# A two-layer mLSTM, attention and RWKV-7 trunk on one core: values mixed behind the 16x16 inverse, odd chunks and state products in the other column half

## The chip, the core and the metric

The kernel runs on one core of a Trainium2 chip. Its engines are TensorE (PE, with its weight loads as PEld), VectorE (DVE), ScalarE (ACT), GpSimd (POOL) and SyncE (SP), which here mainly issues DMAs. The metric is the device time of one execution in microseconds, as the median of several runs.

## What is computed

Two layers, each of one input projection, three branches and one output projection, on 512 tokens of 2048 features in float32:

```python
for l in range(2):
    h = rms_norm(x, norm_g[l]);  proj = h @ w_in[l]
    y_ml  = mlstm(4 heads of 128, chunks of 64)      # from columns mq mk mv mo mz
    y_mla = low-rank attention(8 heads of 128 + 64)  # from columns cq ck az
    y_rw  = rwkv7(8 heads of 64)                     # from columns rr rk rv rz and "misc"
    x = x + concat(silu(z) * y for the three) @ w_out[l]
return rms_norm(x, final_norm_g)

# the branch that is changed:
def step(S, inp):                 # per head, S is 64x64
    rt, wt, kt, vt, at, bt = inp
    sa = einsum('bhvk,bhk->bhv', S, at)
    S = S * wt + sa * bt + vt * kt
    return S, einsum('bhvk,bhk->bhv', S, rt)
v = v if l == 0 else v + (v_first - v) * sigmoid(v0 + (v @ v1) @ v2)
y = head_layer_norm(y) + sum(r * k * r_k) * v
```

## The kernel before

Projections and their fill. The input projection of a layer is 26 blocks of 256 columns (`ORDER`, `gemm`, L239; L235 for mv). Each float32 weight tile is split by ACT and DVE into a high and a low part (`wsplit`, L150 and L151), and three passes of 128x128 by 512 columns (256 for mv) are summed. The results go to DRAM (`park`) and are fetched again by their users. `Work.along` calls one step of these projections for every step (`yield`) of a branch, so that the branches' code and the projections' code alternate; the order of each engine's instructions is then made when the program is built, by a scheduler that simulates it. Inside `with in_order()` PE's instructions keep the order of the code. On the chip each engine runs its queue strictly in that order.

Pairs. `rw_pair(p)` handles two of the eight RWKV heads, in eight chunks of 64 tokens, four pairs a layer. It makes decays and keys; a head sum psbo (L714) for the bonus term bv; on POOL the products bk (L785); the values v, in layer 1 mixed with those of layer 0 by a product psv2, a sigmoid and a second fetch; their transposes psTv into UV; the transposes psTa into AR; the 64x64 products psG and transposes psTk into GG. The lower triangular 64x64 matrices of the chunks are then inverted. The 16x16 diagonal blocks are inverted on DVE, reached through two DMA round trips (`inv_d`), which ends with T32 and X32 (L898, L903). Then 32x32 blocks: psQ and psT (L913, in `prod32`), psQ and psX again (L940, L949), each a group of small PE matmuls, an evacuation by ACT or DVE, and the next group. psR (L842) is issued with the first psQ. psW, psM, psN and psY (L842, L851) make the pair's state terms.

Small tiles. A matmul whose operands are 32 or 64 rows and columns uses a tile of PE: rows by where the operands start, columns by where the output starts. `prod32` and `prod` use the tiles on the diagonal. `cross` sends the odd chunks to the other column half and therefore into a second PSUM bank; before, psR, psW and psM are made so.

States and heads. After the pairs, `rw_states` runs the recurrence over chunks (psS, L995), then for each pair the product psYl (L1015), the norm and the transposes psTy. It alternates with `ml_head(0)` and `ml_head(1)` of the mLSTM branch (psSm L1085, psN L1099, psHT L1130). `ml_head(2)` and `ml_head(3)` alternate with the attention's low-rank steps (psrck, psrcq). Then attention (`HEADS`: psqr, psqn, pskn, psv, pssc, pspt, pso) and the output projection (po, L1390).

PSUM has eight banks by tag: two "a" (`bank`), two "b" (`bank2`, of which a head's psN holds both), three "g" (projections), one "h" (`bank3`).

Of the kernel before, what the change touches and what calls it, by code (L numbers as in the profile page):

```python
# [73 lines left out]
def trunk(ctx, tc, a, out):  # L74
    nc = tc.nc
# [441 lines left out]
    for l in range(DEPTH):  # L517
# [176 lines left out]
        def rw_pair(p, l=l):  # L694
# [13 lines left out]
            def head_sum(x, tag, name):  # L708
# [3 lines left out]
                ps = bank(f"{name}{nm}")  # L712
# [47 lines left out]
            ps = head_sum(bo, "AR", "psbo")  # L760
# [3 lines left out]
            v = fetch("rv")  # L764
            if l > 0:
                bg.ensure("rv1")
                ps = bank(f"psv2_{nm}")
                mm(ps, lhsT=v2[:, p * 128:(p + 1) * 128], rhs=kept["vv"], start=True, stop=True)
                yield
                s = tmp("vs")  # L770
                sigm(s, ps, pch(R_V0 + p))
                vf = tmp("vf")
                dma(vf, vf_d[p])
                tt(vf, vf, v, ALU.subtract)
                tt(vf, vf, s, ALU.mult)
                tt(v, v, vf, ALU.add)
            tt(bv, bv, v, ALU.mult)
            dma(tail_d[p, 0], bv)
# [11 lines left out]
            def token_major(blocks, dst, nn, bank_=bank):  # L790
# [5 lines left out]
                for par in range(2):  # L796
                    for h in range(2):
# [5 lines left out]

            UV = rp.tile([128, 2, 8, 64], F32, tag="UV", name=f"UV{nm}")
            token_major(lambda tb: v[:, tb * 128:(tb + 1) * 128], lambda h: UV[hs[1 - h], h], "v")
            AR = rp.tile([128, 8, 128], F32, tag="AR", name=f"AR{nm}")
            token_major(lambda tb: ar[:, 0, 2 * tb:2 * tb + 2, :].rearrange("p c n -> p (c n)"),
                        lambda h: AR[hs[h], :, 0:64], "a", bank2)
# [17 lines left out]
            for half in range(2):  # L826
                ps = bank(f"psTk{half}{nm}")
                for c in range(4):
# [3 lines left out]
                    GG[:, :, half * 4:half * 4 + 4, 128:192], ps.rearrange("p (c h n) -> p h c n", h=2, n=64))  # L832
            yield
            def cross(n, lhs, rhs, name, banks_):
# [4 lines left out]
                for c in range(0, 8, 2):  # L839
                    for odd in (1, 0):  # L840
# [64 lines left out]
            for _ in range(3):  # L905
                yield

            def prod32(lhs, rhs, name):
                ps = bank(f"{name}{nm}")
                pv = ps[:, 0:256].rearrange("p (c n) -> p c n", n=32)  # L910
                for c in range(8):
                    for n, q in enumerate(q4):
                        mm(pv[q, c, :], lhsT=lhs(q, c, n), rhs=rhs(q, c), start=True, stop=True)  # L913
                return pv

            def blk(m):
                return lambda q, c, e=0: m[q, c, :]
            Q = small([128, 8, 32], "Q", "Qa")
            with in_order():
                psQ = prod32(lambda q, c, n: GG[q, n // 2, c, n % 2 * 32:n % 2 * 32 + 32], blk(T32), "psQ")  # L920
# [620 lines left out]
```

## Time and profile before

| | us |
|---|---|
| median of 3 runs | 1999.47 (1997.14 to 2000.08) |
| the profiled execution | 2003.1 |
| its span, first to last instruction | 2001.4 |
| PE busy | 1953.5 (98%) |
| DVE busy | 1234.5 (62%) |
| ACT busy | 861.5 (43%) |
| POOL busy | 136.2 (7%) |

Busy is the share of the span in which an engine had an instruction in work. Matmuls overlap with their successors, so what a matmul costs is the distance from its start to the next one's. The granted clock of PE stands in the slices of the page and in each window. A wait is the idle time of an engine ahead of an instruction, with the instruction that ended it.

### The profile page before, as it was taken

What the parts mean: (1) busy time and instruction counts of PE and PEld (TensorE: products, weight loads), DVE (VectorE), ACT (ScalarE), POOL (GpSimd) and SP (SyncE); (2) the same over time, 40 slices, a digit from 0 to 9 for tenths busy, and PEclk for the clock granted to TensorE, in tenths of its full rate; (3) what the DMA queues carried; (4) which work ended last, traced back from release to release, by engine and by line L of the source; (5) the groups of instructions that cost most, each with busy time, mean ns of one, the idle gap of its engine ahead of it and who ended that gap; (6) DMA issues with size and microseconds to landing.
All of it is one profiled execution on the core that took longest, in us unless ns stands there. A gap on an engine that the chain in (4) does not pass through costs nothing.

```text
span 2001.4 us, 31675 instructions
## 1 busy us (share of the span) xinstructions
PE 1953.5 (98%) x12544; PEld 1622.1 (81%) x12544; DVE 1234.5 (62%) x2115; ACT 861.5 (43%) x1483; POOL 136.2 (7%) x168
## 2 busy tenths in 40 slices
PE   8999999999999999999999999999999998799998
PEld 6888888888888878888887788888888877687886
DVE  6864867575666499533365458567664768785343
ACT  6534343434546355323353234242423566554233
POOL 4010101100000021000001001010100001110000
PEclk9999999999999999999999999999999999899999
DMA  5443434335555443344444443434345555233334
GB/s 175 136 132 115 121 117 127 111 106 169 162 177 173 124 118 122 101 137 135 144 116 135 127 111 117 127 117 132 109 121 163 169 172 168 76 121 122 116 116 158
DMA packets 246393, 264.86 MB, mean 132 GB/s; under 512 B 49972, under 2 KB 178174, under 8 KB 246246
## 3 DMA queue, kind: packets, MB, share of 16 engines
q1 hardware_dynamic: 245398, 261.88, 42.9%
q8 instruction: 98, 1.61, 0.3%
q0 software_dynamic: 848, 0.97, 0.2%
q14 instruction: 49, 0.40, 0.1%
HBM read 212.45 MB, written 50.35 MB: 131 GB/s over the span
## 4 chain that ended last, share of the span: by engine, by line
PE 87%; DVE 6%; DMA 2%; issue 2%; ACT 2%; SPq 0%; ACTq 0%; DVEq 0%
PE po L1390 17%; PE pg_az L239 7%; PE pg_rr L239 4%; PE pg_mo L239 4%; PE pg_rz L239 4%; PE pg_rk L239 4%; PE pg_rv L239 4%; PE pg_mz L239 4%; PE pg_cq L239 4%; PE pg_mv L235 4%; PE pg_mq L239 3%; PE pg_mk L239 3%; PE pssc L1311 2%; PE pg_ck L239 2%; PE pg_misc L239 2%
## 5 line engine op out<-in xcount | busy, mean ns | idle before, releaser
L1390 PE MATMUL po<-whi_o,mh 128*128 128x512 f32 x512 | 200.3, 391 | 0.1
L1390 PE MATMUL po<-whi_o,ml 128*128 128x512 f32 x512 | 199.4, 389 | 0.0
L151 DVE TENSOR_TENSOR wlo_o<-raw_o,whi_o 128x1024 fp32r<-128x1024 f32 x64 | 78.3, 1224 | 188.4 <-ACT whi_o L150 187.3
L1390 PE MATMUL po<-wlo_o,mh 128*128 128x512 f32 x512 | 187.8, 390 | 0.0
L150 ACT ACTIVATE whi_o<-raw_o 128x1024 fp32r<-128x1024 f32 x64 | 67.7, 1059 | 204.6 <-PE po L1390 166.3
L1390 PEld LDWEIGHTS po<-whi_o,mh 128*128 128x128 f32 x512 | 96.1, 188 | 20.5 <-DVE Vl L254 0.6
L1390 PEld LDWEIGHTS po<-wlo_o,mh 128*128 128x128 f32 x512 | 96.1, 188 | 19.9
L1390 PEld LDWEIGHTS po<-whi_o,ml 128*128 128x128 f32 x512 | 96.1, 188 | 19.6
L239 PE MATMUL pg_az<-xh,whi_az 128*128 128x512 f32 x256 | 101.5, 397 | 0.0
L239 PE MATMUL pg_az<-xl,whi_az 128*128 128x512 f32 x256 | 100.9, 394 | 0.0
L239 PE MATMUL pg_az<-xh,wlo_az 128*128 128x512 f32 x256 | 100.0, 396 | 0.0
L235 PE MATMUL pg_mv<-wlo_mv,xh 128*128 128x256 f32 x256 | 73.2, 286 | 1.4 <-DVE wlo_mv L151 1.4
L235 PE MATMUL pg_mv<-whi_mv,xl 128*128 128x256 f32 x256 | 72.9, 285 | 0.0
L235 PE MATMUL pg_mv<-whi_mv,xh 128*128 128x256 f32 x256 | 72.6, 284 | 0.0
L785 POOL TENSOR_TENSOR bk<-kk,Ei 64x512 f32<-64x512 f32 x16 | 27.5, 1717 | 443.3 <-DVE E L730 230.6
L239 PEld LDWEIGHTS pg_az<-xh,wlo_az 128*128 128x128 f32 x256 | 48.5, 190 | 9.7
L239 PEld LDWEIGHTS pg_az<-xh,whi_az 128*128 128x128 f32 x256 | 48.6, 190 | 9.6
L239 PEld LDWEIGHTS pg_az<-xl,whi_az 128*128 128x128 f32 x256 | 48.6, 190 | 9.5
L151 DVE TENSOR_TENSOR wlo_az<-raw_az,whi_az 128x1024 fp32r<-128x1024 f32 x32 | 39.1, 1222 | 20.6 <-ACT whi_az L150 20.3
L239 PE MATMUL pg_rk<-xl,whi_rk 128*128 128x512 f32 x128 | 51.6, 404 | 0.0
L239 PE MATMUL pg_rk<-xh,whi_rk 128*128 128x512 f32 x128 | 51.0, 402 | 0.5 <-ACT xh L252 0.5
L239 PE MATMUL pg_cq<-xh,whi_cq 128*128 128x512 f32 x128 | 51.2, 400 | 0.0
(572 smaller groups left out, 5548.9 us busy)
## 6 DMA issues: line engine op xcount, KB each, us to landing
raw_o<-in_w_out_dram SPq DMA_DIRECT2D x64, 512.0 KB
raw_az<-in_w_in_dram SPq DMA_DIRECT2D x32, 512.0 KB
raw_rk<-in_w_in_dram SPq DMA_DIRECT2D x16, 512.0 KB
raw_rr<-in_w_in_dram SPq DMA_DIRECT2D x16, 512.0 KB
raw_rv<-in_w_in_dram SPq DMA_DIRECT2D x16, 512.0 KB
raw_rz<-in_w_in_dram SPq DMA_DIRECT2D x16, 512.0 KB
raw_mq<-in_w_in_dram SPq DMA_DIRECT2D x16, 512.0 KB
raw_mk<-in_w_in_dram SPq DMA_DIRECT2D x16, 512.0 KB
```

The lines of the kernel that those rows point to most:

```text
L150: act(hi, raw, AF.Copy)
L151: (nc.gpsimd if name[0] == "u" or name in ("misc0_0", "misc0_1") else nc.vector).tensor_tensor(lo, raw, hi.bitcast(F32), ALU.subtract)
L235: mm(ps[u][:, (tb % 2) * 256:(tb % 2) * 256 + 256], lhsT=xx[:, sl], rhs=w[:, i, :], start=(k == 0 and n == 0 and tb % 2 == 0), stop=(k == ...
L239: mm(ps[u], lhsT=w[:, i, u * 128:(u + 1) * 128], rhs=xx, start=(k == 0 and n == 0), stop=(k == 15 and n == 2))
L785: nc.gpsimd.tensor_tensor(bk[q, :, slot, :], x[q].rearrange(c64, t=64), Ei[q].rearrange(c64, t=64), ALU.mult)
L1311: mm(ps[:, 0:n], lhsT=x1[:, ts_], rhs=x2[:, 0:n], start=(j == 0), stop=(j == 5))
L1390: mm(pss[tb], lhsT=xx[:, sl], rhs=w, start=(k == korder[0] and j == 0), stop=(k == korder[15] and j == 2))
```

## The change

- The value fetch, the layer 1 value mix, bv times v, and the transposes psTv move from ahead of bk to behind the 16x16 inverse (behind the first `flip()`). psTa moves behind psTk.
- psbo is put into the bank of tag "h" instead of "a".
- `prod32` becomes `cross32`: the odd chunks go to the column half that their row half doesn't use, in a second bank. The evacuations are split into even and odd chunks; the odd ones move between partition halves, for psT through a tile "back".
- psQ and psX of the second 32x32 step likewise, their evacuation now half on ACT and half on DVE.
- psYl, before on the diagonal, likewise, with a "b" bank for the odd chunks, in the order of chunks 2, 1, 4, 3, 6, 5, 7, inside `in_order()`.
- psW issues even chunks before odd ones.

```diff
-            ps = head_sum(bo, "AR", "psbo")
+            ps = head_sum(bo, "AR", "psbo", bank3)
             yield
             bv = tmp("bv")
             nc.scalar.copy(bv, ps)
-            v = fetch("rv")
-            if l > 0:
...
-            tt(bv, bv, v, ALU.mult)
-            dma(tail_d[p, 0], bv)
...
-            UV = rp.tile([128, 2, 8, 64], F32, tag="UV", name=f"UV{nm}")
-            token_major(lambda tb: v[:, tb * 128:(tb + 1) * 128], lambda h: UV[hs[1 - h], h], "v")
...
             flip()
-            for _ in range(3):
+            yield
+            v = fetch("rv")
+            if l > 0:
+                bg.ensure("rv1")
+                ps = bank(f"psv2_{nm}")
+                mm(ps, lhsT=v2[:, p * 128:(p + 1) * 128], rhs=kept["vv"], start=True, stop=True)
                 yield
...
+            UV = rp.tile([128, 2, 8, 64], F32, tag="UV", name=f"UV{nm}")
+            token_major(lambda tb: v[:, tb * 128:(tb + 1) * 128], lambda h: UV[hs[1 - h], h], "v")
+            for _ in range(2):
+                yield
...
+            def cross32(rows, lhs, rhs, name, banks_, order=(1, 0)):
+                pv = [b_(f"{name}{o}{nm}")[:, 0:128].rearrange("p (c n) -> p c n", n=32) for o, b_ in enumerate(banks_)]
+                for c in range(0, 8, 2):
+                    for o in order:
+                        for i, j in rows:
+                            mm(pv[o][q4[j ^ 2 * o], c // 2, :], lhsT=lhs(i, c + o), rhs=rhs(i, c + o),
+                               start=True, stop=True)
                 return pv
...
-            tt(Q, psQ, mq.rearrange("p a b -> p (a b)")[:, None, :].broadcast_to([128, 8, 32]), ALU.mult)
+            for j in range(2):
+                tt(Q[hs[j], odd, :], psQ[1][hs[1 - j]], mqb[hs[1 - j]], ALU.mult)
+            tt(Q[:, even, :], psQ[0], mqb, ALU.mult)
...
-            psT_ = prod32(blk(X32), blk(Q), "psT32")
-            tt(T32, psT_, T32, ALU.add)
+            with in_order():
+                psT_ = cross32(four, lambda i, c: X32[q4[i], c, :], lambda i, c: Q[q4[i], c, :], "psT32", (bank, bank))
+            back = small([128, 4, 32], "back")
+            for j in range(2):
+                nc.scalar.copy(back[hs[j]], psT_[1][hs[1 - j]])
+            tt(T32[:, even, :], psT_[0], T32[:, even, :], ALU.add)
+            tt(T32[:, odd, :], back, T32[:, odd, :], ALU.add)
...
-            for h in range(2):
-                nc.scalar.copy(Q[q4[2 * h + 1]], pv[q4[2 * h + 1]])
+            for j in (1, 3):
+                nc.scalar.copy(Q[q4[j], odd, :], psQ[1][q4[j ^ 2]])
+                nc.vector.tensor_copy(Q[q4[j], even, :], psQ[0][q4[j]])
...
-                psY = bank(f"psYl{nm}").rearrange("p (c n) -> p c n", n=64)
-                for c in range(1, 8):
-                    for q in hs:
-                        mm(psY[q, c, :], lhsT=Yl[q, c, :], rhs=DNa[q, c - 1, p, :], start=True, stop=True)
+                psY = [b_(f"psYl{o}{nm}").rearrange("p (c n) -> p c n", n=64) for o, b_ in enumerate((bank, bank2))]
+                with in_order():
+                    for c in (2, 1, 4, 3, 6, 5, 7):
+                        for h, q in enumerate(hs):
+                            mm(psY[c % 2][hs[h ^ c % 2], c, :], lhsT=Yl[q, c, :], rhs=DNa[q, c - 1, p, :],
+                               start=True, stop=True)
```

How this moves instructions, at four places. The names are tile, pair or head, and a buffer number.

PE at layer 1's entry into attention, before: pg_az is the layer's last projection, psHT_2 belongs to mLSTM head 2, psrcq to the low-rank queries.

```order
L239 MATMUL pg_az_15726<-xh_15_8291,wlo_az_3_15791 128x512
L1248 MATMUL psqr_0_15868<-cqh_0_14934,whi_uqr_0_15821 128x512
...
L1248 MATMUL psqr_0_15868<-cqh_3_14937,wlo_uqr_0_15822 128x512
L1130 MATMUL psHT_2_15162<-idf,hn_2_15157 128x128
L1203 MATMUL psrcq_15055<-ones,cqr_1_15049 128x1 x4
L1130 MATMUL psHT_2_15162<-idf,hn_2_15157 128x128 x3
L1248 MATMUL psqn_0_15902<-cqh_0_14934,whi_uqk_0_15864 128x512
```

The same place after the change, here with head 3's transposes (psHT_3).

```order
L239 MATMUL pg_az_15974<-xl_13_8429,whi_az_3_16038 128x512
L1145 MATMUL psHT_3_15555<-idf,hn_3_15550 128x128
L239 MATMUL pg_az_15974<-xh_13_8413,wlo_az_3_16039 128x512
L1145 MATMUL psHT_3_15555<-idf,hn_3_15550 128x128 x3
L239 MATMUL pg_az_15974<-xh_14_8414,whi_az_3_16038 128x512
...
L239 MATMUL pg_az_15974<-xh_15_8415,wlo_az_3_16039 128x512
L1263 MATMUL psqr_0_16116<-cqh_0_15182,whi_uqr_0_16069 128x512
```

Head 2's end and all of head 3 stood behind the last projection; now both heads end ahead of it, with six projections between head 3 and psqr.

PE between the head sum psbo and psG in pair 1 of layer 0, before.

```order
L714 MATMUL psbo_1_1807<-psbox_1_1804,bones 128x512
L794 MATMUL psTv_1_1842<-idf,xrv_1_1830 128x128 x4
L714 MATMUL psbo_1_1807<-psbox_1_1804,bones 128x512
L239 MATMUL pg_mq_2523<-xh_0_132,whi_mq_0_2426 128x512
L239 MATMUL pg_mq_2523<-xl_0_148,whi_mq_0_2426 128x512
```

And after.

```order
L714 MATMUL psbo_1_1746<-psbox_1_1743,bones 128x512
L239 MATMUL pg_rv_2355<-xh_8_140,whi_rv_2_2435 128x512
L797 MATMUL psG_1_1807<-ar_1_1732,bk_1_1769 128x128
L797 MATMUL psG_1_1806<-ar_1_1732,bk_1_1769 128x128
L797 MATMUL psG_1_1807<-ar_1_1732,bk_1_1769 128x128
```

psTv has left the place between psbo and psG, and psG, which stood 22 projections later, follows psbo directly.

PE at the second 32x32 step (psQ) of pair 0 in layer 0, before: one bank, one row of 16.

```order
L239 MATMUL pg_rr_1861<-xl_2_150,whi_rr_0_1765 128x512
L239 MATMUL pg_rr_1861<-xh_2_134,wlo_rr_0_1766 128x512
L239 MATMUL pg_rr_1861<-xh_3_135,whi_rr_0_1765 128x512
L940 MATMUL psQ_0_1524<-T_0_1332,GG_0_1178 32x32 x16
L239 MATMUL pg_rr_1861<-xl_3_151,whi_rr_0_1765 128x512
```

And after, with one buffer number for the odd and one for the even chunks.

```order
L239 MATMUL pg_rk_1671<-xl_5_153,whi_rk_1_1675 128x512
L919 MATMUL psQ_0_1447<-T_0_1202,GG_0_1060 32x32 x2
L919 MATMUL psQ_0_1446<-T_0_1202,GG_0_1060 32x32 x2
L919 MATMUL psQ_0_1447<-T_0_1202,GG_0_1060 32x32 x2
L919 MATMUL psQ_0_1446<-T_0_1202,GG_0_1060 32x32 x2
```

The 16 matmuls stand in one uninterrupted group as before, odd and even chunks by turns.

DVE at the first psQ of pair 3 in layer 1, before: wlo is the low part of a projection's weights.

```order
L151 TENSOR_TENSOR wlo_cq_0_14645<-raw_cq_0_14612,whi_cq_0_14644 128x1024
L923 TENSOR_TENSOR Qa_3_12751<-psQ_3_12754,mq 128x256
L926 COPY AR_3_12547<-psR_3_12788 64x4x64
L542 TENSOR_TENSOR sg_cq_0_14660<-pg_cq_14550,rb_9554 128x512
L929 TENSOR_TENSOR T_3_12697<-psT_3_12822,T_3_12697 128x256
L903 STREAM_TRANSPOSE X_3_12698<-T_3_12697 128x256
```

And after.

```order
L151 TENSOR_TENSOR wlo_mo_3_14597<-raw_mo_3_14564,whi_mo_3_14596 128x1024
L931 TENSOR_TENSOR Qa_3_12854<-psQ_3_12858,mq 64x4x32 x2
L932 TENSOR_TENSOR Qa_3_12854<-psQ_3_12857,mq 128x4x32
L935 COPY AR_3_12713<-psR_3_12892 64x4x64
L942 TENSOR_TENSOR T_3_12766<-psT_3_12941,T_3_12766 128x4x32
L943 TENSOR_TENSOR T_3_12766<-back_3_12976,T_3_12766 128x4x32
L886 STREAM_TRANSPOSE X_3_12767<-T_3_12766 128x256
```

One operation on psQ became three, one on psT two, behind the same kind of wlo operation.

## Rows read from the trace of the kernel before

**Rows 1.** The page: busy us (share of the span) by engine; granted clock in slices.

```profile
PE 1953.5 (98%) x12544; PEld 1622.1 (81%) x12544; DVE 1234.5 (62%) x2115; ACT 861.5 (43%) x1483; POOL 136.2 (7%) x168
PEclk9999999999999999999999999999999999899999
```

**Rows 2.** The page: the chain that ended last, shares by engine.

```profile
PE 87%; DVE 6%; DMA 2%; issue 2%; ACT 2%; SPq 0%; ACTq 0%; DVEq 0%
```

**Rows 3.** Windows: start:end, length, busy (instructions) PE PEld DVE ACT POOL, clock, DMA.

```profile
698.00:747.00 49.00, 45.79 (x253) 38.65 (x252) 45.03 (x90) 28.37 (x62) 15.04 (x9) 0.97 0.43 122
1673.00:1749.00 76.00, 59.03 (x310) 47.68 (x309) 60.29 (x131) 44.99 (x99) 15.48 (x9) 0.89 0.38 116
...
1640.00:1652.00 12.00, 9.04 (x41) 7.39 (x40) 8.55 (x14) 7.12 (x11) 0.00 (x0) 0.72 0.48 155
```

**Rows 4.** Timeline of PE at both layers' entry into attention: start us, length.

```profile
698.18 0.39 PE L239 MATMUL pg_az<-xl,whi_az 128*128 128x512 f32 x1
698.41 0.39 PE L239 MATMUL pg_az<-xh,wlo_az 128*128 128x512 f32 x1
698.63 0.39 PE L1248 MATMUL psqr<-cqh,whi_uqr 128*128 128x512 f32 x1
...
746.92 0.39 PE L1248 MATMUL psqn<-cqh,whi_uqk 128*128 128x512 f32 x1
...
1673.21 0.39 PE L239 MATMUL pg_az<-xh,wlo_az 128*128 128x512 f32 x1
...
1748.98 0.39 PE L1248 MATMUL psqn<-cqh,whi_uqk 128*128 128x512 f32 x1
```

**Rows 5.** Waits of PE: us in total, times, longest.

```profile
PE psv L1276 <- DVE qrf L1221: 5.0, 2, 2.6
PE pskn L1248 <- DVE Vl L254: 4.4, 1, 4.4
PE psHT L1130 <- DVE hn L1126: 3.6, 1, 3.6
...
PE psT L913 <- DVE Qa L923: 2.7, 3, 1.1
PE psN L1099 <- DVE mel L254: 2.2, 1, 2.2
...
PE psrck L1175 <- ACT cksq L1170: 0.7, 1, 0.7
```

**Rows 6.** Timeline of PE in layer 0, head 3; 12 psN stand from 641.67.

```profile
640.86 0.95 PE L1203 MATMUL psrcq<-ones,cqr 128*128 128x1 f32 x8
641.67 0.31 PE L1099 MATMUL psN<-mvh,meh 128*128 128x130 f32 x1
...
643.04 0.39 PE L1085 MATMUL psSm<-mqh,mkh 128*128 128x384 f32 x1
```

**Rows 7.** Timeline of weight loads, four groups of small tiles: start, length, passes.

```profile
156.38 0.64 PEld L913 LDWEIGHTS psQ<-T,GG 32*32 32x32 f32 x64 [0.35 <-issue]
...
157.06 0.56 PEld L842 LDWEIGHTS psR<-UV,GG 64*64 64x64 f32 x32
...
165.09 0.58 PEld L940 LDWEIGHTS psQ<-T,GG 32*32 32x32 f32 x32 [0.35 <-DVE wlo_rr L151]
...
527.35 0.90 PEld L1015 LDWEIGHTS psYl<-DN,Yl 64*64 64x64 f32 x28 [0.17 <-issue]
```

**Rows 8.** Groups by line: busy us, mean ns of one, idle ahead.

```profile
L923 DVE TENSOR_TENSOR Qa<-psQ,mq 128x256 f32<-128x256 f32 x8 | 3.4, 421 | 2.0 <-PE psQ L913 2.0
...
L961 DVE COPY UV<-psW 64x256 f32<-64x256 f32 x8 | 3.3, 418 | 5.8 <-ACT UV L960 5.8
...
L151 DVE TENSOR_TENSOR wlo_o<-raw_o,whi_o 128x1024 fp32r<-128x1024 f32 x64 | 78.3, 1224 | 188.4 <-ACT whi_o L150 187.3
```

**Rows 9.** Timeline of POOL and PE in pair 2 of layer 0: start, length.

```profile
304.78 3.85 POOL L785 TENSOR_TENSOR bk<-kh,Ei 64x512 f32<-64x512 f32 x2
...
309.13 0.39 PE L714 MATMUL psbo<-psbox,bones 128*128 128x512 f32 x1
```

More of the change, by code (lines that the diff above doesn't have):

```diff
@@ L706, in rw_pair, with head_sum @@
             inv_d = inv_ds[p]
-            def head_sum(x, tag, name):
+            def head_sum(x, tag, name, bank_=bank):
                 hl = rp.tile([128, 2, T], F32R, tag=tag, name=f"{name}x{nm}")
                 split2(hl[:, 0], hl[:, 1], x)
-                ps = bank(f"{name}{nm}")
+                ps = bank_(f"{name}{nm}")
                 for u in range(2):
@@ L839, in cross @@
                 for c in range(0, 8, 2):
-                    for odd in (1, 0):
+                    for odd in order:
                         for h in (1, 0):
@@ new lines, in rw_pair @@
+            v = fetch("rv")
[3 more added lines that the diff above has]
+                mm(ps, lhsT=v2[:, p * 128:(p + 1) * 128], rhs=kept["vv"], start=True, stop=True)
+                yield
+                s = tmp("vs")
+                sigm(s, ps, pch(R_V0 + p))
+                vf = tmp("vf")
+                dma(vf, vf_d[p])
+                tt(vf, vf, v, ALU.subtract)
+                tt(vf, vf, s, ALU.mult)
+                tt(v, v, vf, ALU.add)
@@ L918, in rw_pair @@
+            four = [(i, i) for i in range(4)]
             Q = small([128, 8, 32], "Q", "Qa")
+            mqb = mq.rearrange("p a b -> p (a b)")[:, None, :].broadcast_to([128, 4, 32])
             with in_order():
-                psQ = prod32(lambda q, c, n: GG[q, n // 2, c, n % 2 * 32:n % 2 * 32 + 32], blk(T32), "psQ")
+                psQ = cross32(four, lambda i, c: GG[q4[i], i // 2, c, i % 2 * 32:i % 2 * 32 + 32],
+                              lambda i, c: T32[q4[i], c, :], "psQ", (bank, bank))
@@ L929, in rw_pair @@
-            tt(T32, psT_, T32, ALU.add)
+            for j in range(2):
+                tt(Q[hs[j], odd, :], psQ[1][hs[1 - j]], mqb[hs[1 - j]], ALU.mult)
+            tt(Q[:, even, :], psQ[0], mqb, ALU.mult)
+            nc.scalar.copy(AR[:, even, 64:128], psR[0])
+            nc.scalar.copy(AR[hs[0], odd, 64:128], psR[1][hs[1]])
+            nc.vector.tensor_copy(AR[hs[1], odd, 64:128], psR[1][hs[0]])
+            yield
+            with in_order():
+                psT_ = cross32(four, lambda i, c: X32[q4[i], c, :], lambda i, c: Q[q4[i], c, :], "psT32", (bank, bank))
@@ L957, in rw_pair @@
             with in_order():
-                W = cross(128, lambda h, c: X[hs[h], c, :], lambda h, c: AR[hs[h], c, :], "psW", (bank, bank2))
-            even, odd = slice(0, 8, 2), slice(1, 8, 2)
+                W = cross(128, lambda h, c: X[hs[h], c, :], lambda h, c: AR[hs[h], c, :], "psW", (bank, bank2), (0, 1))
             nc.scalar.copy(UV[hs[0], 0, odd, :], W[1][hs[1], :, 64:128])
```

62 lines of the change are left out of this document (21 added, 41 removed).

## The prediction

> **What bounds the kernel now.** I read the page's first lines, then the chain that ended last, then TensorE (PE) by stretch and the waits of PE. PE is busy 98% of the span and holds 87% of the chain [rows 1, 2]: a projection matmul of 512 columns follows the one before it every 0.227 us (698.18, 698.41, 698.63 in [rows 4]), and the work of a head pair stands between such matmuls, so that its latency costs nothing while projections are left to issue. Two things can therefore shorten the time: fewer PE nanoseconds in the pair work itself, and PE waits where the projections have run out. The reader should look for the second first. Both layers enter attention with the same work: from the last projection matmul (az) to the fourth group psqn. In layer 0 that is 698.41 to 746.92, 48.51 us; in layer 1 it is 1673.21 to 1748.98, 75.77 us [rows 4]. The stretch of layer 1 has PE idle for 17.0 of 76 us against 3.2 of 49 us in layer 0, and a mean granted clock of 0.89 against 0.97 [rows 3]: between its two levels, 2.4 and 1.2 GHz, 0.89 means about 17 of 76 us at the lower one. The long waits are named: 4.4 us for Vl, 3.6 us for hn, once each, and for qrf 5.0 us in two places, one in each layer [rows 5]. The first two are there because heads 2 and 3 of the mLSTM branch still run when layer 1 has no projection left; the 57 more matmuls of that stretch [rows 3] are theirs.
>
> **The change, part by part. 1: the order at the end of layer 1.** The counts in this part are matmuls in the order in which the program stands, which the ordered rows ahead of this text show in pieces. Before, 494 projection matmuls of layer 1 stand behind the last state product (psY) of its last pair; none is left at head 2's psHT, so head 2's end and all of head 3 stand among the attention's first products. After, 709 are left at that psY, 154 at head 2's psHT and 7 at head 3's. So 215 matmuls, 215 x 0.227 = 49 us of cover, move from the pairs to the stages behind them. The reason is the value mix: psTv no longer takes one of the two "a" banks between the head sum and psG, and in layer 1 its fetch, product, sigmoid and second load no longer stand ahead of the inverse. The shorter pair chain is itself worth nothing, since PE never starved there; what it leaves over is worth the hole.
>
> The price of the hole: 75.77 - 48.51 = 27.3 us. Not all of it goes, because the heads' own matmuls still have to be issued, now among projections. At the paces of layer 0 [rows 6]: psN 12 in 643.04 - 641.67 = 1.37 us, so 30 take 3.4; the 12 psSm have 3840 columns, at 0.227 us per 512 that is 1.7; psrcq 8 in 0.81; the 8 transposes psHT, at psN's pace, 0.9, and about 0.3 for entering and leaving. Sum 7.1. The gain is 27.3 - 7.1 = 20.2 us, if layer 1 then enters attention as layer 0 does; its PE order and its VectorE (DVE) order there are now those of layer 0, but for 6 projections instead of 128 between psHT and psqr. So the qrf wait stays (2.6 us, in both layers), and up to the 3.6 us of hn [rows 5] may come back because head 3's last DVE steps are nearer. Bounds 16 to 22.
>
> **2: the waits inside layer 1's az stretch.** From 1640 to 1652 PE is busy 9.0 of 12 us at a clock of 0.72 [rows 3]: waits of 0.7 us for cksq and 2.2 us for mel [rows 5], and then matmuls at the lower clock, which fell after that idle time; about 4.8 us together (2.9 idle; some 6.7 us at 1.2 GHz, of which I count 3.8 as work that took twice as long, 1.9). This work is reordered, and layer 0's stretch of this kind has no such wait. Nothing in the order says that it stays or goes: I take half, 2.4 us, bounds 0 and 4.8.
>
> **3: tiles.** A matmul that uses 64 or 32 columns of PE leaves room beside it. The weight loads give the pace [rows 7], with an estimated 0.1 us taken off each row for its last load: psYl, two 64x64 tiles, (0.90 - 0.1)/27 = 30 ns a pass; psR, four tiles because its odd chunks go to the other column half, (0.56 - 0.1)/31 = 15 ns; psQ of the second 32x32 step (L940), two tiles, 15.5 ns; the first psQ (L913), four tiles on the diagonal, 8.6 ns. (Each matmul stands as two passes.) So psQ and psX of the second step, 32 passes each, save 32 x 6.9 = 0.22 us, 16 times: 3.5 us. psYl saves 28 x 15 = 0.41 less 0.06, as chunks 5 and 7 go alone: 0.35, 8 times: 2.8 us. The first psQ and psT go from four tiles to eight, which no row shows: between nothing (the pace is then that of issue) and half of 64 x 8.6 ns, 0.27 us. I take 0.05, near nothing, since the rows show no pass under 8.6 ns; 16 times: 0.8, bounds 0 and 4.3. Sum 7.1 us. The entries into small tiles are as many as before, 93, in the order.
>
> The pair psR and psYl speaks for this: same shape, same two row halves, only the columns differ, and the pace halves. The Trainium skill (TensorE: Matmul & The Clock Gate, Part 3: Packing small matmuls) says that a weight load overlaps with matmuls in flight only when its row group differs. The exchanged chunks share their row group with the others, so by that rule this part would be worth 0 and the sum 7.1 us less; the trace disagrees, at 15 against 30 ns.
>
> **4: what is added.** The first Q was one DVE operation of 421 ns and is now three of half the length; rows of 418 ns for 64 partitions and 421 ns for 128 [rows 8] say that partitions don't matter. A half-length one costs between 0.21 and 0.42 us; I take 0.3, so 0.9 instead of 0.42. Queued behind it on DVE are the psR copy and then T; PE's psT waits for it. Between psQ and psT stand psR and 5 projections instead of 6: 0.6 + 1.1 us. psT waited 2.7 us in 3 of 8 pairs, behind a wlo operation of 1.2 us on DVE [rows 5, 8]. Those 3 get 0.5 + 0.2 us longer, 2.1 us; all 8 would be 5.6, none 0. The T, Q and X copies that are split further are hidden by 20 to 31 projections (over 4 us) at each next step; without that cover they would cost 0.4 to 0.8 us each, 24 times. psYl's second bank is one of the two that a head's pso holds: it stands behind that head's hn, and head 1's psN behind all psYl; the order fills both with projections. 0.4 us, bounds 0 and 2. Moving the fetch of values puts its load later on SP's queue, and psTv stands 47 or more projections ahead of psR in 7 of the 8 pairs (26 in the other, 5.9 us against four copies of 0.4): hidden. psG now follows the second psbo, and needs POOL's bk products; these end at 308.63 where psbo stands at 309.13, the closest of the eight pairs [rows 9], so psG doesn't wait. DVE gets about 2 us a pair, 17 us on 1234 [rows 1]: no bound. Sum +2.5 us.
>
> **Sum.** -20.2 - 2.4 - 7.1 + 2.5 = -27.2 us. The profiled execution took 2003.1 us (span 2001.4, 1.7 around it) and lies 3.6 over the median of the three runs, 1999.47; the steps carry over as differences: 1999.5 - 27.2 = 1972.3.
>
> **Rivals.** (a) *Half a hole*: the heads' chains are slower on the chip than the order assumes, and heads 2 and 3 show waits among projections as head 2 did in part 2, 4.8 us each, while eight tiles and part 2 give nothing: -20.2 - 6.2 + 2.5 + 9.6 = -14, 1985 us. For it: that wait exists; against it: layer 0's heads 2 and 3 have none. (b) *The wait comes back whole*: 7 projections after head 3 are too few, and the attention's first products wait for DVE and ACT as before; tiles and waits alone remain, about -5: 1995. Against it: 31 projections (7 us) now stand ahead of psHT, whose wait for hn was 3.6 us, and Vl is reached in the same order as in layer 0. (c) *Columns don't overlap*, as in the rule quoted: the same without the 7.1 us, 1979.4. (d) *Slower*: the evacuations in more pieces become the bound of the pair steps. There are 32 such steps (psT, psQ, psX, psW in 8 pairs); if each waited as long as the longest psT, 1.1 us [rows 5], that is +35, less 2.7 that is there now, against 20.2 + 7.1 gained: +5, 2005 us. It decides from about 0.95 us a step on; against it stand the 20 projections at three of the four. (e) *More than forecast*: all of part 2 goes and eight tiles halve: -33, 1966.
>
> **How the numbers follow.** Forecast 0.68, (a) 0.14, (b) 0.05, (c) 0.04, (d) 0.04, (e) 0.05. The predicted time is 1972.3. The range reaches from (e) to just above (a), 1965 to 1986. About 0.2%, 4 us, is what a measurement of this kernel can tell from no change: faster by more than that 0.92, within it 0.04 (part of (b) and a mild (d)), slower 0.04.
>
> **What would show it.** In the profile after: the stretch from the last az projection to the fourth psqn of layer 1 at 48 to 53 us and its clock near 0.97; no wait for hn or Vl over 1 us there; psYl 28 passes within 0.55 us and the second psQ 32 within 0.4; psT's waits at 3 to 7 us. I am wrong if that stretch still has over 10 us of idle PE, or if PE waits of over 10 us in all appear between psQ and psW.

## The result and the profile after

The changed kernel takes 1965.85 us (median of 4 runs, 1964.04 to 1966.99) against 1999.78 for the kernel before beside it: ratio 0.983, 95% interval 0.9813 to 0.9847, 33.9 us less where 27.2 were forecast. The profiled executions differ by 39.1: the one of before lies 3.6 us over its median, the one of after 1.8 under its own. All steps below are taken between these two executions.

The page of after, first busy time by engine and the granted clock in slices (before in [rows 1]), then the view of the cores (before stands first: its mean clock was not among the rows ahead):

```profile
PE 1932.2 (98%) x12544; PEld 1607.1 (82%) x12544; DVE 1245.6 (63%) x2179; ACT 863.5 (44%) x1509; POOL 136.4 (7%) x168
PEclk9999999999999999999999999999999999999999
```

```profile
core 0: 2001.4 us, clock 0.991
...
```

```profile
core 0: 1962.3 us, clock 0.997
...
```

Span minus PE busy is PE's idle time: 47.9 us before, 30.1 after, so 17.8 of the 39.1 us were idle. PE's busy time fell by 21.3 with the same number of instructions. The tiles are 6.5 of these (by their weight loads, fourth experiment). For the rest: a mean of 0.991 between 2.4 and 1.2 GHz means 2 x 0.009 x 2001 = 36 us at the lower level, 0.997 means 12; the 24 us that are gone were worth up to 12 of busy time. At least 2.8 us have no name.

Windows of after. The columns are start:end, length, busy time (instructions) of PE, PEld, DVE, ACT, POOL, clock, DMA share, GB/s. The first three answer [rows 3], the others are the stages: pairs and heads of layer 0, pairs and heads of layer 1.

```profile
688.00:737.00 49.00, 45.77 (x254) 38.60 (x253) 44.75 (x90) 28.27 (x63) 15.00 (x9) 0.97 0.43 125
1662.00:1711.00 49.00, 45.13 (x254) 37.36 (x254) 44.16 (x91) 29.43 (x65) 15.53 (x9) 1.00 0.45 132
1590.00:1662.00 72.00, 72.00 (x367) 61.16 (x366) 46.64 (x96) 40.44 (x79) 1.28 (x1) 1.00 0.52 155
```

```profile
0.00:449.00 449.00, 439.55 (x3500) 365.25 (x3500) 316.94 (x504) 195.13 (x305) 50.70 (x104) 1.00 0.44 127
449.00:688.00 239.00, 238.70 (x1347) 199.71 (x1346) 143.87 (x278) 122.21 (x221) 1.29 (x1) 1.00 0.54 167
985.00:1463.00 478.00, 476.52 (x3644) 393.36 (x3644) 315.96 (x477) 189.18 (x281) 32.61 (x26) 1.00 0.41 122
1463.00:1662.00 199.00, 199.00 (x1170) 166.03 (x1165) 132.78 (x269) 108.57 (x204) 1.28 (x1) 1.00 0.55 173
```

The same stages of before, which the rows ahead of the prediction did not hold:

```profile
0.00:467.00 467.00, 455.67 (x3567) 378.77 (x3568) 313.78 (x479) 197.38 (x304) 50.73 (x104) 1.00 0.43 126
467.00:698.00 231.00, 229.79 (x1276) 191.28 (x1275) 138.87 (x270) 114.75 (x206) 1.29 (x1) 0.99 0.53 166
996.00:1524.00 528.00, 527.48 (x3872) 436.50 (x3872) 325.59 (x466) 198.94 (x285) 32.42 (x26) 1.00 0.42 121
1524.00:1673.00 149.00, 146.04 (x875) 121.01 (x876) 102.38 (x206) 85.44 (x156) 1.30 (x1) 0.98 0.56 175
```

The reader should see two things. Layer 1 now enters attention like layer 0: 254 matmuls in 49 us, the clock at 1.00, and the az stretch ahead of it has no idle time at all (72.00 of 72). And work changed its stage in layer 1: the pairs went from 528 to 478 us, the heads and az from 149 to 199, because projections that had filled the pairs now fill the heads. PE in the timeline at that entry, as in [rows 4] (start, length):

```profile
1662.05 0.39 PE L239 MATMUL pg_az<-xh,wlo_az 128*128 128x512 f32 x1
1662.28 0.39 PE L1263 MATMUL psqr<-cqh,whi_uqr 128*128 128x512 f32 x1
...
1710.21 0.39 PE L1263 MATMUL psqn<-cqh,whi_uqk 128*128 128x512 f32 x1
```

The stretch that took 75.77 us takes 48.16 (layer 0 before: 48.51). The waits of PE, where [rows 5] had Vl 4.4, hn 3.6, mel 2.2 and cksq 0.7, have none of these left:

```profile
PE psv L1291 <- DVE qrf L1236: 5.0, 2, 2.6
...
PE psT L919 <- DVE Qa L931: 1.1, 1, 1.1
...
PE psqn L1263 <- POOL wlo_uqk L151: 0.7, 1, 0.7
PE psTk L808 <- DVE GG L801: 0.6, 1, 0.6
```

The weight loads of the small tiles, as in [rows 7], in the order first psQ (eight tiles now), second psQ, psYl:

```profile
137.27 0.64 PEld L919 LDWEIGHTS psQ<-T,GG 32*32 32x32 f32 x64 [0.35 <-issue]
...
146.73 0.34 PEld L919 LDWEIGHTS psQ<-T,GG 32*32 32x32 f32 x32 [0.35 <-issue]
...
510.01 0.56 PEld L1025 LDWEIGHTS psYl<-DN,Yl 64*64 64x64 f32 x28 [0.17 <-issue]
```

0.58 became 0.34 and 0.90 became 0.56; the first psQ stayed at 0.64. And the split evacuation on DVE, as in [rows 8], the odd pieces and the even one:

```profile
L931 DVE TENSOR_TENSOR Qa<-psQ,mq 64x128 f32<-64x128 f32 x16 | 4.6, 288 | 4.0 <-PE psQ L919 3.8
...
L932 DVE TENSOR_TENSOR Qa<-psQ,mq 128x128 f32<-128x128 f32 x8 | 2.3, 292 | 0.3
```

### The profile page after: what moved, and what is told of

Its sections match the earlier page's. It is cut to its first block, busy times and chain, and to the rows that moved or that the text cites. A ratio compares the mean times of both kernels' runs of the same rounds, so it can differ in the third digit from the quotient of the medians.

```text
span 1962.3 us, 31796 instructions
## 1 busy us (share of the span) xinstructions
PE 1932.2 (98%) x12544; PEld 1607.1 (82%) x12544; DVE 1245.6 (63%) x2179; ACT 863.5 (44%) x1509; POOL 136.4 (7%) x168
## 5 line engine op out<-in xcount | busy, mean ns | idle before, releaser
L151 DVE TENSOR_TENSOR wlo_az<-raw_az,whi_az 128x1024 fp32r<-128x1024 f32 x32 | 39.1, 1223 | 31.0 <-ACT whi_az L150 30.8
L150 ACT ACTIVATE whi_az<-raw_az 128x1024 fp32r<-128x1024 f32 x32 | 33.7, 1053 | 39.7 <-PE pg_az L239 26.6
```

What stands on the lines that cost most here:

```text
L150: act(hi, raw, AF.Copy)
L151: (nc.gpsimd if name[0] == "u" or name in ("misc0_0", "misc0_1") else nc.vector).tensor_tensor(lo, raw, hi.bitcast(F32), ALU.subtract)
```

## The experiments

The theory is the prediction's: what is worth time is how many projection matmuls are left in layer 1's order behind the last pair, its cover; the tiles are a small gain beside it. The rivals are that the exchanged tiles carry the gain, and that the gain sits in the pairs themselves. The table sums up what the runs below showed. Each ratio is against runs of the kernel before taken beside that kernel (medians 1999.78 to 2001.65). "Left" are projection matmuls behind layer 1's last psY, head 1's, head 2's and head 3's psHT in the order; the entry is the distance from layer 1's last az projection to head 4's psqn in the timeline; idle is window length minus PE busy in layer 1's pairs, heads and entry.

| kernel | left | median us | ratio, 95% | entry | idle |
|---|---|---|---|---|---|
| before | 494, 151, 0, 0 | 1999.78 | | 75.77 | 0.5, 3.0, 17.0 |
| after | 709, 318, 153, 6 | 1965.85 | 0.983 (0.9813 to 0.9847) | 48.16 | 1.5, 0.0, 3.9 |
| mix alone | 712, 440, 294, 134 | 1972.83 | 0.986 (0.9847 to 0.9874) | 48.40 | 2.4, 0.1, 3.9 |
| tiles alone | 472, 48, 0, 0 | 2012.6 | 1.0058 (1.0045 to 1.007) | 96.57 | 2.7, 0.0, 25.4 |
| columns not exchanged | 709, 318, 153, 6 | 1975.65 | 0.987 (0.9855 to 0.9885) | 48.37 | 1.6, 0.0, 4.0 |
| four round trips | 564, 144, 0, 0 | 1999.14 | 0.9989 (0.9977 to 1.0002) | 71.46 | 12.2, 1.1, 14.0 |
| six round trips | 448, 31, 0, 0 | 2033.12 | 1.0154 (1.0139 to 1.0169) | 101.68 | 16.2, 0.0, 24.0 |
| transposes alone | 609, 299, 142, 8 | 1998.11 | 0.999 (0.9979 to 1.0002) | 47.35 | 9.4, 5.6, 2.9 |
| psbo in tag a | 680, 250, 90, 0 | 1981.13 | 0.99 (0.9884 to 0.9917) | 52.26 | 1.8, 0.2, 5.5 |

### 1. The value mix alone

```diff
-            ps = head_sum(bo, "AR", "psbo")
+            ps = head_sum(bo, "AR", "psbo", bank3)
...
-            v = fetch("rv")
...
             flip()
+            yield
+            v = fetch("rv")
...
```

(The kernel before with the moves of the change, psTv and psTa among them; tiles as before.)

> The kernel before with the value mix alone moved (value fetch, mix, psTv behind the 16x16 inverse, psTa behind psTk, psbo in the bank of tag h); all 32x32 steps and psYl as before, on the diagonal in one bank. In its order 712 projection matmuls are left behind layer 1's last psY, 294 at head 2's psHT and 134 at head 3's, against 494, 0, 0 before and 709, 153, 6 after. Theory (cover: the move of the values leaves projections over, and these fill the hole at layer 1's entry into attention): last az projection to fourth psqn of layer 1 at 48 to 50 us, no wait for hn or Vl; only the tile part is missing, 16 x 0.24 + 8 x 0.34 = 6.5 us, so 1965.9 + 6.5 = 1972. Rival A (the exchanged tiles are needed, since they also shorten the pairs' chain): hole of 10 us or more remains, 1980 to 1990. Rival B (the tiles carry most): within 0.2% of the kernel before.

1972.83 us, ratio 0.986: 28.3 us of the 33.9, with the hole gone. Windows of layer 1's pairs, heads and entry:

```profile
991.00:1471.00 480.00, 477.64 (x3655) 395.34 (x3654) 307.21 (x451) 188.59 (x274) 32.58 (x26) 1.00 0.42 121
1471.00:1671.00 200.00, 199.91 (x1151) 167.16 (x1151) 129.97 (x264) 105.96 (x197) 1.30 (x1) 1.00 0.56 174
1671.00:1719.00 48.00, 44.10 (x248) 36.59 (x247) 43.82 (x87) 28.02 (x62) 15.18 (x9) 1.00 0.42 121
```

The entry has 3.9 us of idle as after, at a clock of 1.00. The time is where the theory put it; both rivals fall.

### 2. The tiles alone

```diff
-            ps = head_sum(bo, "AR", "psbo", bank3)
+            ps = head_sum(bo, "AR", "psbo")
...
+            v = fetch("rv")
...
```

(The changed kernel with the moves undone; tiles exchanged.)

> The changed kernel with the value mix, psTv, psTa and psbo put back to their places before; the tile exchange (both 32x32 steps, psYl, psW's order) stays. In its order 472 projections are left behind layer 1's last psY and none at head 2's psHT, as before the change. Theory (cover): the hole stays, 74 to 78 us from the last az projection to the fourth psqn with waits for hn and Vl; second psQ and psX at 0.38 us and psYl at 0.63 us, so 6.5 us below the kernel before: 1993. Rival A (the exchange brings the gain by a shorter chain): 1975 or less. Rival B (evacuations in pieces cost what the tiles give): 1999, no difference.

2012.6 us, ratio 1.0058, 1.0045 to 1.007: slower than before, which no side had expected. The tiles go at their new pace (second psQ and psX 0.38 us to the next projection, psYl 0.63), and layer 0 does gain: its last az stands at 692.88, 5.5 us earlier than before. Layer 1 loses more. Its heads and its entry:

```profile
1527.00:1659.00 132.00, 132.00 (x810) 108.92 (x809) 88.59 (x177) 70.96 (x130) 1.83 (x1) 1.00 0.57 178
1659.00:1755.00 96.00, 70.63 (x354) 58.32 (x353) 67.61 (x162) 57.53 (x127) 14.26 (x9) 0.79 0.36 108
```

25.4 us of idle and a clock of 0.79 against 17.0 and 0.89 in [rows 3]. In its order 48 projections are left at head 1's psHT instead of 151, so nearly all of head 2 falls into the bare stretch, and not its end alone (354 matmuls for 310). That the tiles are 6.5 us faster and the kernel 11 us slower is the theory's mechanism in the other direction; my number for it, 1993, assumed that the hole keeps its size. It isn't the faster pace that uses up the cover: the kernel of the fourth experiment has the old pace and, in layer 1, the counts of the changed kernel. From the last psY to head 1's psHT the order spends 272 projections with the mix alone and 391 with the tiles as well; the first 32x32 step isn't the reason (391 in the third experiment too), and which of the second banks, the split evacuations and the fixed order is, was not run apart.

### 3. The first 32x32 step on the diagonal

```diff
-                psQ = cross32(four, lambda i, c: GG[q4[i], i // 2, c, i % 2 * 32:i % 2 * 32 + 32],
-                              lambda i, c: T32[q4[i], c, :], "psQ", (bank, bank))
+                psQ = prod32(lambda q, c, n: GG[q, n // 2, c, n % 2 * 32:n % 2 * 32 + 32], blk(T32), "psQ")
...
-                psT_ = cross32(four, lambda i, c: X32[q4[i], c, :], lambda i, c: Q[q4[i], c, :], "psT32", (bank, bank))
+            psT_ = prod32(blk(X32), blk(Q), "psT32")
```

> The changed kernel with only the first 32x32 step (first psQ and psT) back on the diagonal: four tiles, one bank, one evacuation each on DVE. Theory (four tiles already go at the pace of issue, 8.6 ns a pass): psQ with psR still 1.31 us, psT still 0.68 us, nothing gained by eight tiles; without the split evacuations psT's waits are 0 to 2 us in all, as after; 1965 to 1967, no difference. Rival A (eight tiles are faster by some 0.05 us a group, as I had forecast, or more): 1967 to 1970. Rival B (three DVE operations in place of one cost PE time): faster than after by 2 us or more.

1964.55 us, ratio 0.9818 (0.9805 to 0.9831): no difference to the changed kernel. The weight loads of psT, four tiles:

```profile
139.78 0.64 PEld L928 LDWEIGHTS psT<-Qa,X 32*32 32x32 f32 x64 [0.37 <-issue]
```

The same 0.64 us as with eight. So the eight tiles gave nothing, and the three DVE operations in place of one cost nothing that the runs can tell: rival (d) of the prediction has no price at this step. The split copies of the later steps were not run by themselves.

### 4. The second bank without the other columns

```diff
-                            mm(pv[o][q4[j ^ 2 * o], c // 2, :], lhsT=lhs(i, c + o), rhs=rhs(i, c + o),
+                            mm(pv[o][q4[j ^ to * o], c // 2, :], lhsT=lhs(i, c + o), rhs=rhs(i, c + o),
...
-                            mm(psY[c % 2][hs[h ^ c % 2], c, :], lhsT=Yl[q, c, :], rhs=DNa[q, c - 1, p, :],
+                            mm(psY[c % 2][q, c, :], lhsT=Yl[q, c, :], rhs=DNa[q, c - 1, p, :],
```

(`to` is 0 for the second psQ and psX.)

> The changed kernel, but the odd chunks of the second psQ, of psX and of psYl go to the second bank in the same column half as the even ones; the number of evacuations, their engines and the banks are those of the changed kernel. Tells the column half from the bank. Theory (the column half makes the pace): psQ and psX back to 0.62 us to the next projection, psYl to 0.96 us, 15.5 and 30 ns a pass; 16 x 0.24 + 8 x 0.34 = 6.5 us above the changed kernel, 1972. Rival (the second PSUM bank makes the pace, the columns nothing): psQ and psX at 0.38, psYl at 0.63, 1966.

1975.65 us, ratio 0.987. The weight loads of the second psQ and of psYl:

```profile
146.49 0.58 PEld L919 LDWEIGHTS psQ<-T,GG 32*32 32x32 f32 x32 [0.35 <-issue]
...
510.88 0.89 PEld L1025 LDWEIGHTS psYl<-DN,Yl 64*64 64x64 f32 x28 [0.17 <-issue]
```

Both are back at the old pace, with two banks and the same evacuations. So the column half makes the pace, and a second bank alone gives nothing; the other columns within one bank were not run. PE busy is 1939.9 against 1932.2: 7.7 us, of which 16 x 0.24 + 8 x 0.34 = 6.5 are these groups. The median lies 9.8 us over the changed kernel's, 3 more than expected; the order of layer 0 differs a little too (281 projections are left at its head 2's psHT, not 320), and PE there has a wait of 1.2 us (psSm for me) that the changed kernel doesn't have. I did not take the rest apart.

### 5 and 6. A longer chain with no PE work

```diff
+            for n in range(4 if l else 0):
+                dma(far_ds[n], A16)
+                A16 = small([64, 16, 16], "A16", f"A16{n}_")
+                dma(A16, far_ds[n])
             both = small([64, 2, 512], "TX")
```

(That is the first kernel; the second has 6 for 4.)

> The changed kernel, with four more DMA round trips (store to DRAM and load back of the 16x16 blocks, nothing computed) ahead of the inverse in each pair of layer 1: the pair's chain is longer and no PE instruction is added. In its order 564 projections are left behind layer 1's last psY, 144 at head 1's psHT, 0 at head 2's (before: 494, 151, 0; after: 709, 318, 153). Theory (cover alone sets the hole): the distance from the last az projection to head 4's psqn in layer 1 goes from 48 us back to about 76, as in the kernel before with the same cover at head 1; 7 of these 28 us are heads' work that moves, and waits of 0 to 4 us among the az come back: 1966 + 21 to 25 = 1987 to 1991. Rival (what the change gains in layer 1 is work or waits inside the pairs, not cover): 1966 to 1969.

> The same with six more round trips: 448 projections are left behind layer 1's last psY, 31 at head 1's psHT, none at head 2's; the kernel with the tiles alone has 472, 48 and 0. Theory (cover): the distance from the last az projection to head 4's psqn in layer 1 near that kernel's 97 us and layer 0 as in the changed kernel: 1966 + 49 - 7 + 0 to 4 = 2008 to 2012, slower than the kernel before although all of the change is in it. Rival (not cover): 1966 to 1970.

1999.14 and 2033.12 us. Everything of the change is in these kernels, and the first is as slow as the kernel before, the second 1.5% slower. The entries are 71.46 and 101.68 us, near the 76 and 97 expected. Windows of layer 1's pairs and entry, of the first and the second:

```profile
986.00:1512.00 526.00, 513.84 (x3799) 423.01 (x3799) 328.16 (x489) 196.70 (x289) 32.43 (x26) 0.99 0.42 123
...
1674.00:1745.00 71.00, 56.97 (x300) 45.90 (x298) 56.30 (x122) 40.55 (x90) 15.01 (x9) 0.88 0.39 118
```

```profile
986.00:1546.00 560.00, 543.76 (x3916) 447.84 (x3914) 334.61 (x497) 201.28 (x293) 33.12 (x26) 0.98 0.42 122
...
1671.00:1772.00 101.00, 76.96 (x357) 63.16 (x355) 72.63 (x166) 58.09 (x128) 14.67 (x9) 0.75 0.35 103
```

The medians are 8 and 21 us over the tops of the ranges, and the pairs give most of the reason: 12.2 and 16.2 us of idle there, 1.5 after. One such wait of the first kernel, in the timelines of PE and then of DVE:

```profile
1242.23 0.28 PE L235 MATMUL pg_mv<-whi_mv,xl 128*128 128x256 f32 x1
1246.02 0.58 PE L235 MATMUL pg_mv<-wlo_mv,xh 128*128 128x256 f32 x1 [3.50 <-DVE wlo_mv L151]
```

```profile
1242.69 0.15 DVE L867 TENSOR_TENSOR TX<-A,TX 64x2 f32<-64x2 f32 x1 [6.46 <-DMA A<-far_d]
...
1244.75 1.21 DVE L151 TENSOR_TENSOR wlo_mv<-raw_mv,whi_mv 128x1024 fp32r<-128x1024 f32 x1
```

DVE stands 6.5 us in front of the loaded block, and the low half of the next weights stands behind it in DVE's queue; PE runs out of weights. Without these waits the two would, by an estimate, be near 1999 - 11 = 1988 and 2033 - 15 = 2018. The second is still 6 us over its range; its entry took 101.68 us for the 97 that I had put in. So the cover sets the entry, and a long load ahead of DVE has a price of its own that the count of projections doesn't show.

### 7 and 8. A free bank at the entry

```diff
-            ps = gbank(f"psqr{l}_{hp}")
+            ps = (gbank if hp else bank2)(f"psqr{l}_{hp}")
...
-                ps = gbank(f"psv{l}_{hp}_{tp}")
+                ps = (bank3 if hp == 0 and tp else gbank)(f"psv{l}_{hp}_{tp}")
```

(The second of the two kernels also has the first 32x32 step on the diagonal, as in 3.)

> The changed kernel, with the first psqr of each layer in a bank of tag b and the second half of the first psv in the bank of tag h, both free there, in place of the projections' three banks. psv then needn't wait until DVE has read psqr (2.6 us in each layer); the next wait is psqn of head 1 for the bank of head 0's psqn, which DVE has read at 1674.6, where it starts at 1676.19 in the changed kernel. If it starts as soon as that: 1.5 us a layer, 3 us in all, 1963. Rival (the wait comes back whole at the first pssc, since DVE's order is the same): 1966.

> As the run with free banks at the entry, and with the first 32x32 step back on the diagonal in one bank (four tiles, unsplit evacuations). Theory (four tiles are as fast as eight; the two edits add): 1.5 us a layer off the 1964.6 of that step alone, 1961 to 1962. Rival: no difference to it, 1964 to 1965.

1974.02 and 1976.25 us, ratios 0.9859 (0.9844 to 0.9873) and 0.9871 (0.9856 to 0.9886): both misses, 8 and 12 us slower than without the edit. The first psv of layer 1 starts 2.6 us earlier after the last az projection, and the wait returns at the next step of PE, here in the timeline of the first kernel in layer 1:

```profile
1677.03 0.50 PE L1263 MATMUL psqn<-cqh,whi_uqk 128*128 128x512 f32 x1 [2.52 <-DVE qnl L254]
```

Behind it the order of attention is another one in both layers, with waits that the changed kernel doesn't have (in layer 1 of the first kernel a later psv for qrf 1.9 us, psqn for knl 1.7). Taking away a named wait of 2.6 us moved it and cost more elsewhere.

### 9. The transposes of the values alone

```diff
-            UV = rp.tile([128, 2, 8, 64], F32, tag="UV", name=f"UV{nm}")
-            token_major(lambda tb: v[:, tb * 128:(tb + 1) * 128], lambda h: UV[hs[1 - h], h], "v")
...
             flip()
+            yield
+            UV = rp.tile([128, 2, 8, 64], F32, tag="UV", name=f"UV{nm}")
+            token_major(lambda tb: v[:, tb * 128:(tb + 1) * 128], lambda h: UV[hs[1 - h], h], "v")
```

> The kernel before with one thing of the change: the transposes psTv of the values into UV stand behind the 16x16 inverse; the value fetch, layer 1's mix, psTa, psbo's bank and all tiles are as before. In its order 609 projections are left behind layer 1's last psY, 299 at head 1's psHT, 142 at head 2's, 8 at head 3's (before: 494, 151, 0, 0; mix alone: 712, 440, 294, 134). Theory (cover): enough for the hole, so 48 to 50 us from the last az projection to head 4's psqn in layer 1, and the time of the run with the mix alone, 1973, or up to 3 us above it: 1972 to 1976. Rival (the mix itself has to leave the chain ahead of the inverse): 10 us or more of hole stay, 1983 to 1995.

Half right, and the half that matters is wrong. The entry is 47.35 us, the hole is gone; the time is 1998.11, ratio 0.999 (0.9979 to 1.0002). Windows of pairs, heads and entry of layer 1:

```profile
995.00:1508.00 513.00, 503.62 (x3755) 414.60 (x3754) 316.01 (x458) 192.73 (x279) 32.40 (x26) 1.00 0.41 118
1508.00:1699.00 191.00, 185.36 (x1059) 153.03 (x1056) 124.70 (x257) 105.67 (x195) 1.29 (x1) 0.96 0.52 167
1699.00:1746.00 47.00, 44.08 (x249) 36.44 (x248) 41.59 (x89) 28.35 (x64) 15.48 (x9) 1.00 0.45 131
```

The idle time stands ahead of the entry now: 9.4 us in the pairs and 5.6 among the heads, where the clock falls to 0.96. The longest wait of the pairs, in the timelines of PE and then of DVE:

```profile
1251.04 0.66 PE L827 MATMUL psTk<-idf,bk 128*128 128x128 f32 x4 [3.37 <-DVE GG L820]
```

```profile
1245.43 0.69 DVE L774 TENSOR_TENSOR vf<-vf,xrv 128x512 f32<-128x512 f32 x1 [2.81 <-DMA vf<-vf_d]
...
1250.30 1.28 DVE L820 TENSOR_TENSOR GG<-psG,mar 128x512 f32<-128x512 f32 x2
```

DVE waits 2.8 us for the second load of the value mix, and psG's evacuation, which gives psTk its banks, is queued behind the mix. With the mix behind the inverse this wait cannot stand there. From head 4's psqn in layer 0 to layer 1's last az projection this kernel takes 952.85 us, the mix alone 929.83. The two also differ in psTa's place and psbo's bank. The bank is not the reason: the last experiment has the old bank and takes 927.40 us there. psTa's place was not run by itself. The two waits of psT (4.5 us) and the 5.6 us among the heads I can name but not derive: projections stood behind the waiting matmul in PE's queue, in an order that was fixed when the program was built.

### 10 and 11. The rope later

```diff
-    yield from (("rope", 0), ("in", 0), ("v", 0))
+    yield from (("in", 0), ("rope", 0), ("v", 0))
```

(That is the first kernel; the second has in, v, rope.)

> The changed kernel with the first two steps of attention exchanged: head 0's psqn and pskn before the first psqr, and so DVE's qnl and knl before the five rope operations that psv waited for (2.6 us in each layer). The order of PE and its banks stay those of the changed kernel from head 4 on. Theory: that wait goes, 2 to 5 us in the two layers, 1961 to 1964. Rival (as with the free banks: PE then waits in the first scores for the rope, or elsewhere among heads 0 to 3, for as long): 1965 to 1970.

> The same with psv before the first psqr too: qn, kn, values, rope. Theory as for the rope in second place: 1961 to 1964, with less left to wait for if the rope's result is needed only behind head 1's psqn. Rival: the first scores wait for the rope, which ends later: 1966 to 1970.

1968.28 and 1967.87 us, ratios 0.9837 (0.9824 to 0.985) and 0.9835 (0.9822 to 0.9848): the rival's numbers. In the first kernel the wait of the first psv for qrf (2.6 and 2.4 us) goes. Waits for qrf of 0.9 and 1.1 us stand further on in layer 0 and one of 1.1 in layer 1, and in layer 1 one of 3.8 us for Vh is new, here in the timelines of PE and then of ACT:

```profile
1676.62 0.77 PE L1263 MATMUL psqn<-cqh,whi_uqk 128*128 128x512 f32 x1 [3.77 <-ACT Vh L252]
```

```profile
1670.97 1.26 ACT L252 ACTIVATE mh<-mr 128x512 fp32r<-128x512 f32 x2 [2.63 <-DMA mr<-mix_d]
...
1674.75 0.58 ACT L252 ACTIVATE Vh<-psv 128x512 fp32r<-128x512 f32 x1
```

ACT stands in front of a load for the output projection, with Vh behind it. The second kernel doesn't have that wait, but one of 3.4 us of a later psv for qrf in layer 1.

### 12. psbo alone back in its old bank

```diff
-            ps = head_sum(bo, "AR", "psbo", bank3)
+            ps = head_sum(bo, "AR", "psbo")
```

> The changed kernel with psbo alone put back into a bank of tag a. In its order 680 projections are left behind layer 1's last psY, 250 at head 1's psHT, 90 at head 2's, none at head 3's (after: 709, 318, 153, 6; the run with four round trips: 564, 144, 0, 0). Theory (what PE waits for, stage by stage, is the time; cover at head 3's end decides the entry): some of the hole is back, between the 48 us of the changed kernel and the 71 us of the run with four round trips, 52 to 60 us from the last az projection to head 4's psqn in layer 1, of which half is head 3's work that moves there; 1968 to 1974. Rival (6 projections or none at head 3's psHT make no difference, and the bank gives nothing): 48 to 50 us, 1964 to 1967.

1981.13 us, ratio 0.99 (0.9884 to 0.9917): 15 us for one bank, over the range. The entry is 52.26 us, the lower end of what I expected; most is elsewhere. Layer 0's last az stands at 699.25 against 687.87 after and 698.41 before. The pairs of layer 0:

```profile
0.00:464.00 464.00, 451.12 (x3537) 373.82 (x3539) 318.56 (x504) 196.16 (x310) 50.67 (x104) 1.00 0.43 126
```

12.9 us of idle there and 1.7 among the heads, against 9.4 and 0.3 after. The longest that the changed kernel doesn't have is a psT behind a weight operation of DVE, in the timelines of PE and then of DVE:

```profile
145.72 0.92 PE L919 MATMUL psT<-Qa,X 32*32 32x32 f32 x64 [2.34 <-DVE Qa L931]
```

```profile
143.14 1.22 DVE L151 TENSOR_TENSOR wlo_rk<-raw_rk,whi_rk 128x1024 fp32r<-128x1024 f32 x1
...
144.99 0.59 DVE L931 TENSOR_TENSOR Qa<-psQ,mq 64x128 f32<-64x128 f32 x2
```

All of what the change gained in layer 0 is lost with this one line, the tiles' 3.3 us included. It is not the bank by itself: the kernel with the tiles alone has psbo in the old bank too and gains 5.5 us in layer 0. Why the old bank and the moved values go badly together, no run shows.

None of these kernels beats the changed one by more than the runs differ.

## Why the prediction came out as it did

The range held the time, 0.85 us above its lower end, and the mechanism of layer 1 was right. Terms by the profiled executions:

**Part 1, the hole: right.** 27.6 us of the stretch went, less the 7.1 estimated for the heads' own work: 20.5 for 20.2. That it is the cover, and not the tiles or the chain, is shown by the runs with tiles alone and with four and six round trips, where the hole comes back with the count of projections while the change is wholly or half there. The claim that layer 1 would enter as layer 0 does was exact to 0.4 us.

**Part 2, the waits among the az: taken at half.** All 4.8 us went (72.00 busy of 72). I had no reason for the half but not knowing.

**Part 3, the tiles: 6.5 for 7.1.** psQ and psX 3.8 for 3.5, psYl 2.7 for 2.8, eight tiles nothing for 0.8. Rival (c), that columns don't overlap, falls with the fourth experiment: the row halves and the banks are the same in both kernels, and 0.34 against 0.58 us for the same 32 passes is the columns alone. By the rule weighed there as the prediction read it (the Trainium skill, TensorE: Matmul & The Clock Gate, Part 3: Packing small matmuls) the two would be equal; the measurement decides.

**Part 4, what is added: wrong sign.** The three DVE operations cost 3 x 0.29 = 0.87 us, as estimated (0.9), but psT waited 1.1 us in one pair, where I forecast 2.7 + 2.1 in three. The 2.7 us of [rows 5] were not a property of the step: they went with the operation that stood ahead of Qa on DVE. In the three pairs that waited that was sg_mq, wlo_mv and sg_mk; in the same pairs after it is wlo_mq, sg_mk (the wait of 1.1 us) and wlo_mq. psYl's second bank showed no wait.

**The step that failed** is the sentence "The shorter pair chain is itself worth nothing, since PE never starved there". Layer 0 has no hole to fill, yet its last az stands 10.5 us earlier (687.87 for 698.41): 3.3 are tiles, the other 7 are not in the sum. The windows show 2.8 us less idle up to there (9.4 + 0.3 for 11.3 + 1.2). Before, PE also ran a stretch at its lower clock, after psN had waited 1.2 us at 529.83; at half the pace, these 3.3 us cost 1.7, and the stage of after has none of it:

```profile
531.70:535.00 3.30, 3.30 (x9) 2.63 (x8) 2.41 (x6) 1.87 (x4) 0.00 (x0) 0.50 0.64 218
```

The last 2.7 us I can't name. In layer 0's pairs PE did wait: six times, at most 1.1 us, 4.2 in all; after, twice, 1.4 in all. The size is no accident of one execution of the changed kernel. The eight kernels whose layer 0 is that of the change (two of them with the first step on the diagonal) have the last az between 686.35 and 688.54; the mix alone has it at 692.82, the tiles alone at 692.88, about half of the gain each. Of the kernel before there is one trace. The last experiment shows that psbo's bank, to which I had given no price, can take all of it away.

By stage, measured against what the forecast comes to there: layer 0 up to its last az 10.5 us for 2.3 (half of the tiles less half of what is added); from there to layer 1's last az, where the heads' work came in, a gain of 0.6 for a loss of 2.4; the hole 27.6 for 27.3; the rest 0.3 for nothing. That is 39.1 for 27.2, and layer 0 makes 8 of the 12 between. The medians differ by 5 us less than the two profiled executions, and only so does the time lie inside the range.

**The rivals.** (e) has the right time for a partly wrong reason: part 2 went whole, but the eight tiles did not halve, and layer 0's gain is not in it. That its 1966 meets the measured time is luck. (a) and (b) did not come, but the transposes-alone kernel is (a) in another dress: the hole filled, and the waits back among pairs and heads. What I forecast for that kernel from the cover alone was at least 22 us too low. Cover in the order is needed for the gain; it doesn't suffice.

## What to carry over

Where long independent work fills the waits of chains, count what is left of it at each later stage: time saved in an early chain is paid out at the end, and an edit that makes a step faster but spends more of the fill early can make the kernel slower (here the exchanged tiles alone were 6.5 us faster and the kernel 11 us slower). Keep a load that arrives late out of the queue ahead of an evacuation that PE needs; the wait shows up on PE under the evacuation's name. A single wait of 1 to 3 us in such an order is not a saving that can be booked: four edits against named waits lost 2 to 12 us.

## What the runs showed of the hardware that I had not expected

Two 32x32 or 64x64 matmuls that share their rows overlap when their columns differ: 0.34 against 0.58 us for 32 passes, 0.56 against 0.89 for 28, and a second PSUM bank without other columns changes nothing. Eight 32x32 tiles are no faster than four: 0.64 us for 64 passes with either. A DVE operation of half the length, 128 elements for 256, takes 0.29 us for 0.42, not half.
